# Two more gate blocks by Strassen's algorithm, its products two at a time between the query tiles

## The chip, the cores and the metric

One core of a Trainium2 chip runs the kernel. The metric is device microseconds from start to end of one execution; three runs are given for the kernel before. The core has five engines that work side by side and wait for each other by semaphores: PE (TensorE, matrix products), DVE (VectorE), ACT (ScalarE), POOL (GpSimd) and SP, which issues most of the transfers. Each engine takes its own instructions in the order in which the program gives them.

## The reference

One decoder layer over 256 tokens with a model width of 2048, all in float32. What matters here is the first product and where its columns go:

```
proj = x @ w_in            # 256 x 2048 times 2048 x 15696
q_lat, c_kv, attn_gate, q_idx, k_idx, w_idx, x_rnn, rnn_gate, g_a, g_b = split(proj)
branch_a = (sparse_attention(q_lat, ...) * silu(attn_gate)) @ w_branch_a
branch_b = (rglru(x_rnn) * silu(rnn_gate)) @ w_branch_b
merged   = sigmoid(g_a) * branch_a + sigmoid(g_b) * branch_b
out      = layernorm(ALPHA * x + merged @ w_out)
```

g_a and g_b are the two merge gates, 2048 columns each. The kernel cuts each of them into four blocks of 512 columns, called ga 0 to 3 and gb 0 to 3.

## The kernel before

**Numbers in two parts.** Each float32 operand is split into a high part (a rounded copy, made on ACT by `hi_of`, L106) and a low part (the rest, made on DVE by `lo_of`, L110). A product is three matmuls: high by high, high by low, low by high. x is split once and stays in SBUF as `xs` (16 tiles of 128 rows of the contraction, with 256 high and 256 low columns).

**The weight stream.** All weights pass through one list, `halves`, in pieces of 128 x 1024. `load_to` (L197) gives a piece's transfer to SP; there are four `raw` buffers. `split_to` splits it on ACT and DVE; there are five `hi` and five `lo` buffers. A step of PE asks for splits about five pieces ahead and for loads nine pieces ahead. A buffer comes free when its last reader is done, so a split can't run further ahead than five pieces.

**The order of the work** is written out by hand. `col_jobs` lists the jobs: the rest of qi, ag (attention gate), q (queries), ga 0 to 2, ba (branch A), xr (recurrence input), gb 1 to 3, rg (recurrence gate), bb (branch B); the output product follows. A job of the kinds qi, ag, q, xr, rg makes 128 columns and is run two at a time by `pair`: eight ticks, four in which the high weights meet x (matmuls of 512 columns, L252) and four in which the low weights meet the high part of x (256 columns). A job of the kinds ga, ba, gb, bb is a `chunk`: 16 ticks of six matmuls of 512 columns each (L922 to L924 in `products`), 96 in all. After each tick's matmuls `tick` runs what is due on the other engines: generators sit in an agenda and give up to a later tick at each `yield`. `spawn` puts them there. So attention heads (`head(h)`, spawned 20 ticks after the pair of query tiles it belongs to), drains of PSUM (`evac`, L335 on ACT and L339 on DVE), mask additions on POOL (L509) and the recurrence's `decay` and `roots` all lie beside the weight stream.

**PSUM** has eight banks: four, tag acc, go round among the accumulators of the jobs, and four, tag aux, among everything else (logits, transposes, values).

**What is there of Strassen's algorithm.** ga 3 and gb 0 have the same left operand x, so [ga 3 | gb 0] is taken as a product of 2 x 2 blocks: two halves of the tokens, two halves of the contraction, two column blocks. `quarter_sums` makes the four sums of x's quarters beside ga, `sums` and `split_to` the sums of the weights, `seven_step` runs the seven products within ba 1 to ba 3 in all four aux banks, and `after_s1` and `after_s2` put them together.

**The recurrence.** `decay(n)` for n = 0 to 15 (a tanh and an exp on ACT, then a square on ACT, L759, then a DVE step, L761) starts at tick G0 + 14 + 2n, where G0 is the start of gb 1; `roots(q)` (square roots on ACT, then 16 products on POOL, L770) at G0 + 50 + q. The rg job starts at G0 + 48.

Of the kernel before, what the change touches and what calls it, by code (L numbers as in the profile page):

```python
# [18 lines left out]
P = 128  # L19
# [47 lines left out]

def seven(job):
# [5 lines left out]
            ("ba", 3): ("s2", tuple(range(8)))}.get(job)  # L74

# [7 lines left out]
def layer(ctx, tc, ar, out):  # L83
# [27 lines left out]

    def acc_tile(name):
        return psum.tile([P, 512], F32, name=name, tag="acc", bufs=4)

    def aux_tile(name):
        return psum.tile([P, 512], F32, name=name, tag="aux", bufs=4)

    def slot(name, dt=F32R):
        return big.tile([P, 2 * T], dt, name=name, tag="slot", bufs=16)
# [4 lines left out]
    def gate_tile(name):  # L124
        return gt.tile([P, 2 * T], F32, name=name, tag="gate", bufs=16)
# [26 lines left out]
    causal = const.tile([P, 2, T], F32, name="causal")  # L152
# [12 lines left out]
    for job in jobs:  # L165
# [3 lines left out]
        for pc in range(8 if job[0] in CHUNKS else 2):  # L169
# [5 lines left out]
            halves.append(("w" + job[0], job[1], pc) if job[0] in CHUNKS else ("wt", tiles.index(job), pc))  # L175
    NO = len(halves)
# [4 lines left out]
    def load_to(n):  # L181
        while st["load"] < min(n, len(halves)):
# [7 lines left out]
            raw = wpool.tile([P, 1024], F32, name=f"raw{i}", tag="raw", bufs=4)  # L190
            if kind == "wt":
                src = ar["wt"][a, :, s * 8:(s + 1) * 8, :].rearrange("p k c -> p (k c)")
            elif kind in ("s1a", "s2a"):
# [4 lines left out]
            raws[i] = raw  # L198
# [5 lines left out]
    def sums(i):  # L204

        k, raw = halves[i][1], raws[i]
# [3 lines left out]
    def split_to(n):  # L210
        while st["split"] < min(n, len(halves)):
            i = st["split"]
            kind, k, _ = halves[i]
            if i + 1 < len(halves) and halves[i + 1][0] == "s1a":
# [3 lines left out]
            if NO + 24 <= i < NO + 28:  # L218
                raw = raws.pop(i)
                pieces = []  # L220
                for e in range(2):
                    hi, lo = slot(f"wh{i}_{e}"), slot(f"wl{i}_{e}")
# [5 lines left out]
            else:  # L228
                if kind == "s1b":
                    raw = raws.pop(i - 1)  # L230
                    nc.vector.tensor_sub(raw[:, 512:], form[k], raw[:, :512])
                    src = [(slice(0, 512), form[k]), (slice(512, 1024), raw[:, 512:])]
                elif kind == "s2b":
# [139 lines left out]
    def post_a():  # L373
# [34 lines left out]
        for d in range(2):  # L408
            cT[d] = slot(f"cT{d}")
# [144 lines left out]
    def head(h):  # L554
# [27 lines left out]
        for r in range(2):  # L582
            nc.vector.tensor_scalar(lr[r], lr[r], sm[:, 6 + r:7 + r], None, op0=OP.mult)
# [29 lines left out]
        us[h] = slot(f"ua{h}")  # L613
# [23 lines left out]
    def post_gb(i, pss):  # L637
        for t in range(2):
            g = gates["gb", i, t] = gate_tile(f"gb{i}_{t}")
# [82 lines left out]
    def post_xr(n, ps):  # L722
# [23 lines left out]
        t = ri[n] = slot(f"ri{n}", F32)  # L746
# [5 lines left out]
    def decay(n):  # L752
# [6 lines left out]
        nc.scalar.activation(a2, r, AF.Square)  # L759
# [12 lines left out]
    def post_rg(n, ps):  # L772
# [12 lines left out]
        us[n] = slot(f"ub{n}")  # L785
# [16 lines left out]
    def quarter_sums():  # L802

        x = []
        for j in range(8):
            x.append(gate_tile(f"form{j}"))
# [3 lines left out]
        yield 24  # L810
# [5 lines left out]
        homes = [("qs", "vh"), ("qs", "vl"), ("vh", "vl"), ("bias", "bias", "pa", "pa")]  # L816
        for j in range(4):
            yield 4 if j == 0 else 2
            dst = [p for tag in homes[j] for p in piece(tag, 2, 1 if tag in ("bias", "pa") else 2)]
            first, second = (x[e].rearrange("p (k t) -> p k t", k=2) for e in (j, j + 4))  # L820
            a11, a21, a12, a22 = (v[:, :, c] for v in (first, second) for c in (slice(0, P), slice(P, T)))
            v = [tmp_tile(f"sum{j}_{i}", tag, bufs).rearrange("p (k t) -> p k t", k=2)
# [9 lines left out]
            for i in range(4):  # L832
                lo_of(dst[i][:, :, 1, :], v[i], dst[i][:, :, 0, :])
                for e in range(2):
                    S[i + 1, 2 * j + e] = (dst[i][:, e, 0, :], dst[i][:, e, 1, :])

# [28 lines left out]
    def after_s1():  # L865

        u = {p: att.tile([P, 512], F32, name=f"u{p}", tag="bias", bufs=2) for p in (1, 3)}
        for t in range(2):
            gates["gb", 0, t] = gate_tile(f"gb0_{t}")
        u4, c22 = gates["gb", 0, 0], gates["gb", 0, 1]  # L870
        nc.scalar.activation(u[1], ps7[1], AF.Copy)
# [355 lines left out]
```

## Time and profile before

| | |
|---|---|
| time, median of 3 runs | 1018.04 us (1017.3 to 1018.33) |
| the profiled execution | 1017.16 us; its span, from first to last instruction, 1015.4 us |
| granted TensorE clock | 0.998 of full speed |
| busy over the span | PE 1008.0, DVE 730.9, ACT 569.1, POOL 94.1 us |
| moved by DMA | 205.87 MB, 203 GB/s in the mean |

The profile comes from one execution. A line of it names the source line, the engine, the operation and the tile; matmuls overlap, so their durations are longer than the distance from one start to the next, and it is that distance which adds up to the span. The stages, by the starts of their matmuls: ag from about 65 us, q from 160, ga from 376, ba from 447, xr from 573, gb from 671, rg from 739, bb from 828, the output product from 920.

### The profile page before, as it was taken

The numbers are of one execution on the slowest core, as the hardware profiler recorded it, in microseconds if no ns is written. First come the engines' busy times: TensorE is split into PE (matmuls) and PEld (weight loads), VectorE is DVE, ScalarE is ACT, GpSimd is POOL, SyncE is SP. The second block draws the span as 40 slices with busy tenths as digits, with TensorE's granted clock in tenths as the row PEclk, the third lists the DMA queues.
The fourth block names the chain that finished last, engine by engine and source line by source line (L and its number), as shares of the span: only waits on it lengthen the run. The fifth ranks groups of instructions, "written<-read, shape, count | busy, mean of one in ns | idle before, by whom it ended". The sixth has DMA issues, their size and how long they took to land.

```text
span 1015.4 us, 14822 instructions
## 1 busy us (share of the span) xinstructions
PE 1008.0 (99%) x5344; PEld 870.6 (86%) x5344; DVE 730.9 (72%) x1244; ACT 569.1 (56%) x953; POOL 94.1 (9%) x129
## 2 busy tenths in 40 slices
PE   9999999999999999999999999999999999999997
PEld 8888888899998888888888888888888888888885
DVE  6578885667677766687888688885668875655685
ACT  6566654555555565554555555558866564444452
POOL 0015421110001030000000000000060000000002
PEclk9999999999999999999999999999999999999999
DMA  9755876655565567656776765566745669656652
GB/s 310 255 163 182 296 240 188 200 176 183 173 185 189 177 214 251 187 188 205 220 218 204 228 189 187 189 205 181 207 152 188 206 218 339 197 183 185 202 168 83
DMA packets 62697, 205.87 MB, mean 203 GB/s; under 512 B 6800, under 2 KB 13840, under 8 KB 61600
## 3 DMA queue, kind: packets, MB, share of 16 engines
q1 hardware_dynamic: 59936, 193.23, 60.2%
q0 software_dynamic: 1968, 10.78, 2.9%
q8 instruction: 42, 0.69, 0.3%
q10 hardware_dynamic: 720, 0.92, 0.3%
q14 instruction: 31, 0.25, 0.1%
HBM read 202.77 MB, written 6.32 MB: 206 GB/s over the span
## 4 chain that ended last, share of the span: by engine, by line
PE 99%; DVE 0%; DVEq 0%; issue 0%
PE ps_q L252 17%; PE ps_ag L252 9%; PE ps_xr L252 9%; PE ps_rg L252 9%; PE ps_bb L924 3%; PE ps_bb L923 3%; PE ps_ba L924 3%; PE ps_ba L923 3%; PE ps_ba L922 3%; PE ps_bb L922 3%; PE psq L252 2%; PE ps_qi L252 2%; PE ps_ga L922 2%; PE ps_ga L924 2%; PE ps_gb L922 2%; PE ps_gb L923 2%
## 5 line engine op out<-in xcount | busy, mean ns | idle before, releaser
L110 DVE TENSOR_TENSOR lo<-raw,hi 128x1024 fp32r<-128x1024 f32 x336 | 408.0, 1219 | 234.2 <-ACT hi L106 214.2
L106 ACT ACTIVATE hi<-raw 128x1024 fp32r<-128x1024 f32 x336 | 345.3, 1047 | 128.2 <-PE pso L924 25.3
L252 PE MATMUL ps_q<-xs,hi 128*128 128x512 f32 x512 | 119.0, 390 | 0.0
L252 PEld LDWEIGHTS ps_q<-xs,hi 128*128 128x128 f32 x512 | 95.3, 188 | 19.3
L252 PE MATMUL ps_q<-xs,lo 128*128 128x256 f32 x512 | 69.2, 284 | 0.0
L252 PEld LDWEIGHTS ps_q<-xs,lo 128*128 128x128 f32 x512 | 65.2, 191 | 1.2
L252 PE MATMUL ps_ag<-xs,hi 128*128 128x512 f32 x256 | 60.0, 390 | 0.0
L252 PE MATMUL ps_xr<-xs,hi 128*128 128x512 f32 x256 | 59.6, 390 | 0.0
L252 PE MATMUL ps_rg<-xs,hi 128*128 128x512 f32 x256 | 59.5, 390 | 0.0
L252 PEld LDWEIGHTS ps_xr<-xs,hi 128*128 128x128 f32 x256 | 47.6, 188 | 9.6
L252 PEld LDWEIGHTS ps_rg<-xs,hi 128*128 128x128 f32 x256 | 47.6, 188 | 9.6
L252 PEld LDWEIGHTS ps_ag<-xs,hi 128*128 128x128 f32 x256 | 47.5, 188 | 9.5
L922 PE MATMUL ps_bb<-hi,ub 128*128 128x512 f32 x128 | 50.4, 393 | 0.0
L924 PE MATMUL ps_bb<-hi,ub 128*128 128x512 f32 x128 | 49.9, 390 | 0.0
L923 PE MATMUL ps_bb<-lo,ub 128*128 128x512 f32 x128 | 49.8, 389 | 0.0
L924 PE MATMUL ps_ba<-hi,ua 128*128 128x512 f32 x128 | 49.8, 389 | 0.0
L923 PE MATMUL ps_ba<-lo,ua 128*128 128x512 f32 x128 | 49.8, 389 | 0.0
L922 PE MATMUL ps_ba<-hi,ua 128*128 128x512 f32 x128 | 49.8, 389 | 0.0
L509 POOL TENSOR_TENSOR bias<-bias,mask 128x256 f32<-128x256 f32 (+1 forms) x32 | 24.8, 795 | 195.4 <-DMA bias<-dz 170.3
L922 PE MATMUL ps_ga<-hi,xs 128*128 128x512 f32 x96 | 37.7, 393 | 0.0
L922 PE MATMUL pso<-hi,xs 128*128 128x512 f32 x96 | 37.5, 391 | 0.0
L924 PE MATMUL ps_ga<-hi,xs 128*128 128x512 f32 x96 | 37.4, 390 | 0.0
(358 smaller groups left out, 1971.7 us busy)
## 6 DMA issues: line engine op xcount, KB each, us to landing
raw<-in_wt SPq DMA_DIRECT2D x168, 512.0 KB, 4.8
raw<-in_wba SPq DMA_DIRECT2D x32, 512.0 KB, 3.7
raw<-in_wbb SPq DMA_DIRECT2D x32, 512.0 KB, 4.2
raw<-in_wo SPq DMA_DIRECT2D x32, 512.0 KB, 3.5
raw<-in_wga SPq DMA_DIRECT2D x24, 512.0 KB, 4.5
raw<-in_wgb SPq DMA_DIRECT2D x24, 512.0 KB, 4.5
raw<-in_ws SPq DMA_DIRECT2D x16, 512.0 KB, 4.4
wr<-in_wA SPq DMA_DIRECT2D x14, 424.0 KB, 4.7
```

The costliest lines, as they stand in the source:

```text
L106: nc.scalar.activation(hi, src, AF.Copy)
L110: nc.vector.tensor_sub(lo, src, f(hi))
L252: nc.tensor.matmul(ps[:, :n], w, rhs[:, :n], start=start, stop=stop)
L509: nc.gpsimd.tensor_add(b[:, r, :W[r]], b[:, r, :W[r]], mask[:, r, :W[r]])
L922: nc.tensor.matmul(o, mh, hi, start=first and d == 0, stop=False)
L923: nc.tensor.matmul(o, mh, lo, start=False, stop=False)
L924: nc.tensor.matmul(o, ml, hi, start=False, stop=d == KT - 1)
```

## The change

ga 2 and gb 3 are no longer chunks. [ga 2 | gb 3] is a second product of 2 x 2 blocks with seven products of 24 matmuls (8 tiles of the contraction, three matmuls each). They are run in four phases: j1 (products 1 and 5, eight steps), j2 (3 and 6, eight), j3 (7 alone, four steps of two tiles), j4 (2 and 4, eight). Each step is six matmuls of 512 columns and takes one new piece from the weight stream. `quarters` says after which pair of query tiles the steps stand: none after pairs 0 to 2, two each after 3 to 6, none after 7, then 3, 3, 2, 2, 2, 3, 2, 3 after pairs 8 to 15.

- PSUM: banks get fixed numbers. Banks 3 and 7 are taken out of the two rounds from the end of pair 3 until `after_j4`, one tick into ga; three accumulators and three aux banks are left for the query tiles and the heads.
- x's sums: `early_sums` (three sums, beside pairs 0 to 2) and `late_sum` (the fourth, on POOL, 12 operations, beside pairs 10 to 12). The existing `quarter_sums` moves to ga's now shorter stretch.
- Weight sums: one DVE subtraction of 128 x 512 per step, two in j3.
- Moved between engines: the scaling of the probabilities in `head` from DVE (L583) to ACT, the square in `decay` (L759) from ACT to POOL.
- Moved in time: gb has two chunks, so rg starts at G0 + 32; `decay(n)` starts at G0 + 14 + 4n/3, `roots(q)` at G0 + 37 + q/2.
- The gate tiles and slots are parted into two tags each (gate and form, slot and late); the number of buffers is the same.

```diff
-    jobs += [("ga", i) for i in range(3)] + [("ba", i) for i in range(4)]
+    jobs += [("ga", i) for i in range(2)] + [("ba", i) for i in range(4)]
-    jobs += [("gb", i) for i in range(1, 4)] + [("rg", i) for i in range(16)]
+    jobs += [("gb", i) for i in range(1, 3)] + [("rg", i) for i in range(16)]
...
+def quarters(pair):
+    steps = [("j1", k) for k in range(8)] + [("j2", k) for k in range(8)]
+    steps += [("j3", k) for k in range(4)] + [("j4", k) for k in range(8)]
+    n = (0, 0, 0, 2, 2, 2, 2, 0, 3, 3, 2, 2, 2, 3, 2, 3)
+    return steps[sum(n[:pair]):sum(n[:pair + 1])]
...
+    accs, auxs = [0, 1, 2, 3], [4, 5, 6, 7]
     def acc_tile(name):
-        return psum.tile([P, 512], F32, name=name, tag="acc", bufs=4)
+        accs.append(accs.pop(0))
+        return bank(accs[-1], name)
...
+        if kind == "j1":
+            return nc.vector.tensor_sub(form[k], raw[:, 512:], raw[:, :512])
+        if kind == "j2":
+            return nc.vector.tensor_sub(form[k], raw[:, :512], form[k])
...
-            nc.vector.tensor_scalar(lr[r], lr[r], sm[:, 6 + r:7 + r], None, op0=OP.mult)
+            nc.scalar.activation(lr[r], lr[r], AF.Copy, scale=sm[:, 6 + r:7 + r])
...
-        nc.scalar.activation(a2, r, AF.Square)
+        nc.gpsimd.tensor_mul(a2, r, r)
...
+    def late_sum(j):
+        d, e = (rows2(tmp_tile(f"s3{i}_{j}", "s")) for i in "de")
+        x = [f(xs[:, 2 * j:2 * j + 2, c:c + P]) for c in (0, P, T, T + P)]
+        nc.gpsimd.tensor_sub(d, x[0], x[1])
+        nc.gpsimd.tensor_sub(e, x[2], x[3])
+        nc.gpsimd.tensor_add(d, d, e)
...
+    def quarter_step(job, k):
+        i = where[job, k]
+        split_to(i + 5)
+        load_to(i + 9)
...
+        for e, (p, (mh, ml)) in enumerate(todo):
+            hi, lo = (v[:, e * 512:(e + 1) * 512] for v in parts[i])
+            last = k == (3 if job == "j3" else 7) and (p != 7 or e == 1)
+            nc.tensor.matmul(psj[p], mh, hi, start=k == 0 and (p != 7 or e == 0), stop=False)
+            nc.tensor.matmul(psj[p], mh, lo, start=False, stop=False)
+            nc.tensor.matmul(psj[p], ml, hi, start=False, stop=last)
+        parts.pop(i)
+        split_to(i + 6)
+        load_to(i + 10)
...
+    for j, pair in enumerate((11, 11, 12, 12)):
+        spawn(D0 + 8 * pair - (4 if j < 2 else -1) + j % 2, late_sum(j))
...
-        spawn(G0 + 14 + 2 * n, decay(n))
+        spawn(G0 + 14 + 4 * n // 3, decay(n))
-        spawn(G0 + 50 + q, roots(q))
+        spawn(G0 + 37 + q // 2, roots(q))
...
+        if kind == "q":
+            for job, k in quarters(i // 2):
+                if (job, k) == ("j1", 0):
+                    accs.remove(3)
+                    auxs.remove(7)
+                quarter_step(job, k)
+                if k == (3 if job == "j3" else 7):
+                    spawn(t0 + 8, after[job]())
```

## Rows read from the trace of the kernel before

**Rows 1.** The page: span, busy time of the engines, engines of the chain.

```profile
span 1015.4 us, 14822 instructions
...
PE 1008.0 (99%) x5344; PEld 870.6 (86%) x5344; DVE 730.9 (72%) x1244; ACT 569.1 (56%) x953; POOL 94.1 (9%) x129
...
PE 99%; DVE 0%; DVEq 0%; issue 0%
```

**Rows 2.** Windows q, ba, xr, gb: stretch, length, PE, PEld, DVE, ACT, POOL busy, clock, DMA.

```profile
243.00:296.00 53.00, 53.00 (x327) 47.71 (x326) 37.89 (x89) 30.62 (x70) 4.97 (x8) 1.00 0.59 179
...
469.00:573.00 104.00, 104.00 (x456) 85.47 (x455) 85.50 (x99) 55.32 (x63) 0.00 (x0) 1.00 0.70 213
573.00:678.00 105.00, 105.00 (x622) 93.60 (x621) 85.77 (x146) 58.51 (x97) 1.55 (x16) 1.00 0.61 197
678.00:739.00 61.00, 61.00 (x279) 50.82 (x278) 36.35 (x49) 48.48 (x84) 0.00 (x0) 1.00 0.65 195
```

**Rows 3.** Timeline of PE over gb: start, duration, engine, line, tile.

```profile
670.59 0.40 PE L922 MATMUL ps_gb<-hi,xs 128*128 128x512 f32 x1
...
676.06 0.28 PE L258 MATMUL psg<-xcs,wgh 128*128 128x256 f32 x1
...
676.78 0.39 PE L922 MATMUL ps_gb<-hi,xs 128*128 128x512 f32 x1
...
678.17 0.28 PE L258 MATMUL psg<-xcs,wgh 128*128 128x256 f32 x1
...
738.88 1.29 PE L252 MATMUL ps_rg<-xs,hi 128*128 128x512 f32 x5
```

**Rows 4.** Timeline of PE over one pair of query tiles.

```profile
264.88 7.44 PE L252 MATMUL ps_q<-xs,hi 128*128 128x512 f32 x32
...
272.16 1.11 PE L252 MATMUL ps_q<-xs,lo 128*128 128x256 f32 x8
...
278.06 7.44 PE L252 MATMUL ps_q<-xs,hi 128*128 128x512 f32 x32
```

**Rows 5.** Timeline of DVE around the end of that pair.

```profile
276.50 1.23 DVE L110 TENSOR_TENSOR lo<-raw,hi 128x1024 fp32r<-128x1024 f32 x1 [3.04 <-ACT hi L106]
277.64 0.83 DVE L569 TENSOR_TENSOR bias<-bias,lg 128x128 f32<-128x128 f32 x1
...
281.35 0.41 DVE L339 TENSOR_TENSOR s_q<-ps_q,r_q 128x256 f32<-128x256 f32 x1
```

**Rows 6.** DVE's groups in 199.6 to 358, 160 to 375 and 450 to 573 us.

```profile
L110 DVE TENSOR_TENSOR lo<-raw,hi 128x1024 fp32r<-128x1024 f32 x47 | 57.4, 1228 | 42.7 <-ACT hi L106 39.1 <-PE pspT L588 3.6
...
L583 DVE TENSOR_SCALAR lg<-lg,sm 128x256 f32<-128x256 f32 (+1 forms) x26 | 7.0, 310 | 0.0
...
L110 DVE TENSOR_TENSOR lo<-form,hi 128x512 fp32r<-128x512 f32 x16 | 11.0, 687 | 0.5 <-ACT hi L106 0.3
L208 DVE TENSOR_TENSOR form<-form,raw 128x512 f32<-128x512 f32 x8 | 5.5, 693 | 0.3
```

**Rows 7.** Timeline of DVE and POOL in rg, with and without POOL at work.

```profile
743.34 4.34 POOL L770 TENSOR_TENSOR decay<-decay,ri 128x256 f32<-128x256 f32 x6 [74.85 <-DVE decay L767]
748.93 11.58 POOL L770 TENSOR_TENSOR decay<-decay,ri 128x256 f32<-128x256 f32 x10 [1.25 <-DVE decay L767]
...
755.21 0.96 DVE L780 TENSOR_TENSOR g<-g,s_rg 128x256 f32<-128x256 f32 x1
...
768.10 0.42 DVE L780 TENSOR_TENSOR g<-g,s_rg 128x256 f32<-128x256 f32 x1
```

**Rows 8.** ACT's groups in 693 to 739 us.

```profile
L106 ACT ACTIVATE hi<-raw 128x1024 fp32r<-128x1024 f32 x17 | 17.9, 1054 | 3.5 <-PE ps_gb L924 3.4
L756 ACT ACTIVATE ri<-ri,nc 128x256 f32<-128x256 f32 x16 | 8.2, 510 | 0.5
L755 ACT ACTIVATE decay<-ri,c 128x256 f32<-128x256 f32 x16 | 7.9, 497 | 1.7 <-DVE ri L750 1.7
```

**Rows 9.** The page's DMA issues: size, median us from issue to landing.

```profile
raw<-in_wt SPq DMA_DIRECT2D x168, 512.0 KB, 4.8
```

More of the change, by code (lines that the diff above doesn't have):

```diff
@@ L175, in layer @@
             halves.append(("w" + job[0], job[1], pc) if job[0] in CHUNKS else ("wt", tiles.index(job), pc))
+        if job[0] == "q" and job[1] % 2:
+            for step in quarters(job[1] // 2):
+                where[step] = len(halves)
+                halves.append((*step, 0))
     NO = len(halves)
@@ L197, in load_to @@
             nc.sync.dma_start(raw, src)
-            raws[i] = raw
     form = {}
     def sums(i):
-        k, raw = halves[i][1], raws[i]
+        kind, k, _ = halves[i]
+        raw = raws[i]
+        if kind == "j1":
+            return nc.vector.tensor_sub(form[k], raw[:, 512:], raw[:, :512])
+        if kind == "j2":
+            return nc.vector.tensor_sub(form[k], raw[:, :512], form[k])
+        if kind == "j3":
+            for e in range(2):
+                c = slice(e * 512, (e + 1) * 512)
+                nc.vector.tensor_sub(raw[:, c], form[2 * k + e], raw[:, c])
+            return
+        if kind == "j4":
+            return nc.vector.tensor_sub(raw[:, 512:], form[k], raw[:, :512])
         nc.vector.tensor_sub(raw[:, 512:], raw[:, 512:], raw[:, :512])
@@ L221, in split_to @@
                 for e in range(2):
-                    hi, lo = slot(f"wh{i}_{e}"), slot(f"wl{i}_{e}")
+                    late = i == NO + 27 and e == 1
+                    hi, lo = slot(f"wh{i}_{e}", late=late), slot(f"wl{i}_{e}", late=late)
                     c = raw[:, e * 512:(e + 1) * 512]
@@ L612, in head @@
         yield
-        us[h] = slot(f"ua{h}")
+        us[h] = slot(f"ua{h}", late=h > 13)
         hi_of(us[h][:, :T], u)
@@ L809, in quarter_sums, with four, rows2 @@
                                 ar["xT"][2 * j:2 * j + 2].rearrange("k p t -> p k t"))
-        yield 24
+        return x
+    def four(x, j):
+        first, second = (x[e].rearrange("p (k t) -> p k t", k=2) for e in (j, j + 4))
+        return [v[:, :, c] for v in (first, second) for c in (slice(0, P), slice(P, T))]
+    def rows2(t):
+        return t.rearrange("p (k t) -> p k t", k=2)
+    def quarter_sums():
+        x = load_quarters(1)
+        yield 12
         def piece(tag, bufs, n=1):
@@ new lines, in late_sum @@
+    def late_sum(j):
[4 more added lines that the diff above has]
+        nc.gpsimd.tensor_add(d, d, e)
+        yield 2
+        if j % 2:
+            spare = const.tile([P, 2, T], F32R, name=f"spare{j}", tag="causal", bufs=1)
+            hi, lo = (spare[:, i, :] for i in range(2))
+        else:
+            hi, lo = (ev.tile([P, T], F32R, name=f"s3{i}_{j}", tag="g", bufs=2) for i in "hl")
+        hi, lo = rows2(hi), rows2(lo)
+        hi_of(hi, d)
+        yield
+        lo_of(lo, d, hi)
+        for i in range(2):
+            SJ[3, 2 * j + i] = (hi[:, i, :], lo[:, i, :])
@@ new lines, in after_j4 @@
+    def after_j4():
+        nc.vector.tensor_add(cq["a"], psj[2], cq["a"])
+        yield
+        nc.vector.tensor_sub(cq["b"], cq["b"], psj[4])
+        accs.insert(0, 3)
+        auxs.insert(0, 7)
+        gates["gb", 3, 0], gates["gb", 3, 1] = cq["d"], cq["c"]
+        yield 20
+        for t, n in enumerate("ab"):
+            gates["ga", 2, t] = cq[n]
+            nc.scalar.activation(cq[n], cq[n], AF.Sigmoid)
+            yield
+    after = {"j1": after_j1, "j2": after_j2, "j3": after_j3, "j4": after_j4}
```

147 lines of the change are left out of this document (107 added, 40 removed).

## The prediction

> **What bounds the kernel now.** I read the page first, then the chain of waits, then the windows by stage. The page gives PE 1008.0 us of a span of 1015.4, and the chain that ended last is PE for 99% of its length [rows 1]. The windows say that this is no mean over unlike stages: in q, ba, xr and gb alike PE is busy for the whole stretch and its clock is granted in full [rows 2]. The reader is to see two things in these windows. Time can be won only by taking matmuls away, and any stall put into PE is lost in full. The second thing is how near the others are: DVE fills 71% of q (37.89 of 53.00), and 82% of ba and of xr (85.50 of 104.00, 85.77 of 105.00), and still PE never waits; ACT fills 79% of gb (48.48 of 61.00). So PE's supply holds up to 82% of DVE at least; beyond that this trace shows nothing.
>
> **What PE loses and gains.** The stretch of three gb chunks runs from 670.59 to 738.88, 68.29 us. Four groups of six small matmuls (psg) stand in it, one of them from 676.06 to 676.78, 0.72 us; without them 65.41 us are left for 288 matmuls, 0.2271 us each [rows 3]. Two chunks of 96 go: 192 x 0.2271 = 43.6 us. Added are 28 steps of six such matmuls. Six in a row after a change of form took 1.39 us (676.78 to 678.17) [rows 3], a little more each than in the long run. The steps stand in groups of 12 or 18 after 256-column work, so I take the dearer price: 28 x 1.39 = 38.9 us. The difference is -4.7 us. At the long-run price (168 x 0.2271 = 38.2) it would be -5.4, the best end.
>
> **DVE beside the query tiles.** A pair of query tiles takes 13.18 us (264.88 to 278.06) [rows 4]; at 37.89 of 53.00 us DVE works 9.4 us of it [rows 2]. Moving the scaling to ACT takes off 7.0 us over 13 heads, 0.54 each [rows 6], so 8.9 us. A step of j1 or j2 adds one subtraction of 0.69 us and two low parts of 512 columns at 0.69 [rows 6], 2.1 us against 1.39 us of PE; a step of j4 adds 0.69 and one low part of 1.23, 1.9 us; a step of j3 two subtractions and 1.23, 2.6 us. So a pair with three steps gives DVE 8.9 + 6.2 = 15.1 us in 17.35 of PE (87%). The densest is pair 12: 8.9 + 5.2 for two steps of j3, one closing addition (0.69) and two low parts of the late sums (0.42 each, as a 128 x 256 product without POOL [rows 7]) make 15.6 in 13.18 + 2.78 = 15.96 us (98%). Over pairs 8 to 13 it is six times 8.9, eight steps of j2 (16.6), four of j3 (10.4), three of j4 (5.8), four closing additions (2.8) and four late low parts (1.7): 90.5 of 100.0 us.
>
> **POOL beside DVE.** The late sums and one addition of products put 13 POOL instructions beside pairs 10 to 12. While POOL multiplied in rg, DVE's product on line 780 took 0.96 us; with POOL idle it took 0.42 [rows 7]. So each POOL instruction can cost DVE 0.54 us, 13 of them 7.0, and the dense pairs would stand at 97.5 of 100. The Trainium skill's page "SBUF — State Buffer", section "Who interferes with whom", says that a DVE instruction with two SBUF inputs and a GpSimd instruction that reads SBUF exclude each other for a whole instruction; the trace agrees (0.96 against 0.42). By that rule alone DVE would wait at each meeting, and the result is the first rival below.
>
> Not every one is met. The late sums of tiles 0 and 1 start before DVE's pause (3.04 us in front of the low part at 276.50 [rows 5]); that pause is theirs. Those of tiles 2 and 3 fall at the head of pair 12, where DVE has a queue: six times 0.54, 3.2 us, and 15.6 + 3.2 is 2.9 over PE's 15.96. The splits run up to five pieces ahead, so most of that is taken from the lead. Bounds of the stall that reaches PE in the whole stage: 0 (as at 82%) and 3.7 (first rival). I take 0.7, a quarter of the overrun, nearer to the rows in which PE never waited.
>
> **Three accumulators instead of four.** The second accumulator of a pair is now the bank of the first accumulator of the pair before, and PE wants it half way through the four high ticks, 3.64 us (half of 264.88 to 272.16 [rows 4]) after the pair before has ended, plus 1.39 us per step between. Its drain by DVE starts at 281.35 and takes 0.41 [rows 5]: 3.70 us after the pair's end at 278.06. With no step between (pair 7) that is even, -0.06 us. With two steps PE comes 2.7 us after the drain; with three, one more subtraction and the split low part stand ahead of the drain (0.84 us) and 3.3 us are left. Cost 0.1 us at most; the price without the cover is the second rival.
>
> **ACT, transfers and the queues.** ACT works 30.62 of 53.00 us in q [rows 2], 7.6 per pair; three steps add three high parts at 1.05 [rows 8] and the scaling 0.54 by DVE's row and at most twice that, at most 11.9 of 17.35: hidden. The scaling's result is read three ticks later, where ACT has its own waits. Between three steps and the next pair seven pieces are split in one stretch, but there are four raw buffers and a transfer lands 4.8 us after its issue [rows 9]. The fourth piece of the next pair is wanted 4.17 + 5.5 us after the pair's end, and its buffer comes free 2 to 3 us after it, so it is there with about 2 us over; the stall term holds what of this goes wrong. SP issues the heads' bias loads behind these pieces, a pair ahead of their use; at nothing.
>
> **gb and rg.** From G0 + 14 to G0 + 32 PE has 18 ticks of six matmuls, 24.5 us. In it ACT has 14 decays at 1.01 (0.51 + 0.50) and nine high parts at 1.05 [rows 8], 23.6 us, and the drains of a chunk. It is full but not over, since the square has gone to POOL. What slips goes into the four high ticks of the first rg pair (7.28 us [rows 4], one split), ahead of the roots. I take 0; if that cover is gone, the two decays that no longer fit ahead of rg come first, 2.0 us. Sixteen squares on POOL cost DVE up to 0.54 each in a stretch where it works 36.35 of 61.00 us [rows 2]: hidden.
>
> **The sum.** -4.7 + 0.7 = -4.0 us on the profiled execution of 1017.16, 1013.2. The median of the three runs, 1018.04, lies 0.9 above that execution, so the forecast for a median is 1014.0.
>
> **The rivals.**
> 1. *DVE becomes the bound between pairs 8 and 13, and the gain is spent there.* For it: 90% without POOL, 97.5% with it, and DVE's forced pauses (42.7 us in front of the low parts in twelve pairs [rows 6], 3.6 each, of which some depend on PE and ACT in turn). Against it: these pauses are mostly lead, not need. If 1.2 us of pause per pair stay forced, 97.5 + 7.2 = 104.7 against 100.0; a lead of about 1 us is used up first, so 3.7 are lost: -1.0, about 1017.0.
> 2. *The drain of the first accumulator comes too late at every pair.* PE then waits for DVE, DVE's next work waits for PE, and nothing is caught up. It decides where DVE runs some 3 us later at the end of a pair than now. For it: 0.06 us of shortage without steps, and a stage at 90%. Against it: 2.7 to 3.3 us of room at ten of the eleven seams. At 1 us for each of eleven seams: +11.0 - 4.7 = +6.3, about 1024; above 0.43 us per seam the change loses.
> 3. *ACT is late into rg.* For it: 23.6 of 24.5 us; against it: the quiet high ticks. -4.0 + 2.0, about 1016.0.
>
> **How the numbers follow.** The forecast has 0.68, rival 1 0.15, rival 2 0.10, rival 3 0.07. 0.2% is 2.0 us, about what a measurement can tell here. Faster by more: the forecast and half of rival 3, 0.71. Slower by more: rival 2 and a little of what goes beyond rival 1, 0.11. The rest, 0.18, is within. The range starts at the best end (1018.04 - 5.4) with 0.3 for the spread of runs, 1012.3, and takes in rivals 3 and 1 up to 1018.0; rival 2 and the far end of rival 1 are left out.
>
> **What would show it.** The page has 5320 matmuls (24 fewer), and PE busy about 4 us less. The step groups take 1.39 us per step with no gap. DVE is at 85 to 98% in pairs 8 to 13, and PE's idle time there is under 1.5 us in all: if it is more, the releaser tells rival 1 (a low part, `hi` or `lo`) from rival 2 (the drain `s_q`). The subtraction takes 0.69 us alone. In rg's first two pairs PE has no gap; a gap ended by an ACT high part is rival 3. The forecast is wrong if PE's idle time grows by more than 2 us anywhere, or if the steps take over 1.5 us each.

## The result, and the profile after

The changed kernel takes 1027.49 us in the median of 4 runs (1026.22 to 1028.04), the kernel before 1017.68 beside it: ratio 1.0094, 95% interval 1.0076 to 1.0111. Forecast were 1014.0 us and faster. It is slower, by 9.5 us where 4.0 were to be won. (In the experiments one of the ten runs of `e8_five` took 1482.52 us at a granted clock of 0.632; it is left out, so that the median told here is 1018.60 and not the 1018.96 of the expectations.)

The page of the changed kernel, the lines that answer to [rows 1]:

```profile
span 1025.8 us, 14984 instructions
...
PE 1006.9 (98%) x5320; PEld 867.4 (85%) x5320; DVE 780.7 (76%) x1306; ACT 594.9 (58%) x1014; POOL 127.9 (12%) x166
...
PE 87%; DVE 5%; ACT 4%; issue 2%; DMA 1%; POOL 0%; DVEq 0%; ACTq 0%; POOLq 0%
```

The 24 matmuls are gone, as forecast, and the chain that ended last is no longer PE alone: DVE, ACT and DMA hold a tenth of it. What PE waited for in the changed kernel (in all us, times, longest; the kernel before has none of these seven):

```profile
PE psl L305 <- DVE cq_b L994: 5.2, 1, 5.2
PE pspv L650 <- DVE vl L120: 2.8, 1, 2.8
PE psj L961 <- DVE pb L120: 1.3, 1, 1.3
PE psj L962 <- DVE lo L120: 1.1, 1, 1.1
...
PE ps_rg L299 <- ACT hi L116: 0.6, 1, 0.6
...
PE psj L961 <- ACT hi L116: 0.3, 1, 0.3
PE ps_ga L1096 <- DVE lo L120: 0.3, 1, 0.3
```

Seven waits, 11.6 us. By stage, from the starts of the first matmuls (us); the two columns on the right are experiments told below:

| stage | before | changed | `e14_roots_spaced` | `e18_j3_unsubtracted` |
|---|---|---|---|---|
| q, with the 28 steps | 216.2 | 260.9 | 256.7 | 254.4 |
| ga (3 chunks before, then 2) | 71.2 | 57.2 | 50.1 | 50.1 |
| ba | 126.1 | 126.2 | 126.2 | 126.2 |
| xr | 97.5 | 97.5 | 97.5 | 97.5 |
| gb (3 chunks before, then 2) | 68.3 | 46.5 | 46.5 | 46.5 |
| rg | 88.9 | 90.1 | 90.0 | 89.9 |

gb gives back 21.8 us for one chunk; ga should too and gives 14.0. The price of a step, in the changed kernel's timeline of PE (the answer to [rows 3]): 18 matmuls, three steps, and then the next pair.

```profile
290.57 0.40 PE L961 MATMUL psj<-hi,sj 128*128 128x512 f32 x1
...
294.67 0.62 PE L299 MATMUL ps_q<-xs,hi 128*128 128x512 f32 x2
```

4.10 us, 1.37 per step; 28 steps are 38.3 us. So q should be 216.2 + 38.3 = 254.5 and is 260.9. The losses are 6.4 us in q, 7.8 in ga and 1.3 in rg; 15.5 less the 43.6 - 38.3 = 5.3 of matmuls won is 10.2, and the spans differ by 10.4. Within q the loss lies in three pairs of query tiles: 1.6 us in pair 3, 3.1 in pair 11, 1.9 in pair 12. Each of the other thirteen takes its time of the kernel before and 1.37 us per step, within 0.05 us.

The engines over three stretches of q (the columns of [rows 2]):

```profile
243.00:296.00 53.00, 53.00 (x304) 46.75 (x303) 42.30 (x90) 35.12 (x74) 5.88 (x8) 1.00 0.59 189
296.00:349.00 53.00, 50.25 (x290) 44.31 (x289) 43.48 (x81) 35.15 (x74) 11.32 (x14) 1.00 0.60 186
349.00:402.00 53.00, 51.64 (x295) 45.03 (x295) 45.94 (x88) 32.87 (x67) 11.04 (x11) 1.00 0.61 187
```

DVE is at 80, 82 and 87%. In the first stretch PE never waits, in the second, at 82%, it loses 2.75 us. In the kernel before, PE never waited at 82% in ba and xr [rows 2]. The share does not tell the two apart. By pairs it tells still less; here are pair 11 and pair 13, each with its steps:

```profile
330.57:349.54 18.97, 16.22 (x95) 14.20 (x94) 15.76 (x27) 11.19 (x23) 4.34 (x4) 1.00 0.58 181
...
367.36:384.67 17.31, 17.31 (x100) 15.26 (x99) 16.97 (x35) 11.16 (x23) 2.15 (x2) 1.00 0.62 185
```

With DVE at 83% pair 11 loses 2.75 us; with DVE at 98% pair 13 loses nothing. What tells them apart is the chain. The chain of the changed kernel through pair 11 (start, us, what):

```profile
329.05 2.28 DVE lo L120 x2
...
331.35 5.28 DMA raw<-in_wga
...
336.71 1.29 DVE raw L247 x2
338.01 1.14 DVE lo L120
...
340.47 1.40 DVE qs L120
...
342.21 0.61 DVE vl L120
...
342.86 0.50 PE pspv L650
```

Read backwards: `pspv` wants an aux bank that still holds the values `psv`; the bank is free when DVE has written `vl`; `vl` stands in DVE's queue behind a split, and that behind a subtraction (L247) that waited for its weight piece, which landed 5.28 us after the buffer had come free. DVE's own timeline between 332 us and `vl` at 342.13 says what makes it late: 1.33 and 0.50 us of idle time for two landings, 2.4 us of subtractions for two pieces, and `qs`, which takes 1.48 us beside POOL's addition to `cq_c` where the next `qs` takes 0.41. The chain at the start of ga is of the same kind:

```profile
421.19 7.41 DMA raw<-in_wga
...
428.70 1.06 ACT hi L116
...
429.79 1.23 DVE lo L120
431.02 0.60 DVE cq_a L992
...
432.68 0.61 DVE cq_b L994
...
433.33 0.58 PE psl L305
```

`after_j4` puts bank 7 at the head of the aux round, so head 14's logits (`psl`) get it, and it still holds product 4 until `cq_b` has been written, behind a split that waited for a landing of 7.41 us. What stood beside that landing is in the timelines of POOL and SP in 414 to 434 us:

```profile
416.54 5.82 POOL L855 DMA_DIRECT2D form<-in_xT  x8
```

```profile
416.30 15.07 SPq L229 DMA_DIRECT2D raw<-in_wga  x7
```

x's quarters (2 MB) are sent for beside seven weight pieces. In 420 to 430 us the DMA engines are at a share of 1.00 and move 365 GB/s (177 in the 18 us before).

This burst is not new. The kernel before sends for the same 2 MB at the same place, one tick later in ga (POOL, L808, from 373.60 us). Its weight pieces there take up to 7.1 us to land, and PE does not wait:

```profile
380.00:385.00 5.00, 5.00 (x30) 4.40 (x29) 2.90 (x9) 2.64 (x5) 0.00 (x0) 1.00 1.01 374
385.00:390.00 5.00, 5.00 (x26) 4.08 (x25) 5.00 (x11) 2.91 (x6) 0.35 (x1) 1.00 1.00 343
```

New in the changed kernel is that a bank which PE wants at once is drained behind such a landing.

### The profile page after: what moved, and what is told of

It reads as the page before. It is cut to its first block, busy times and chain, and to the rows that moved or that the text cites. A ratio compares the mean times of both kernels' runs of the same rounds, so it can differ in the third digit from the quotient of the medians.

```text
span 1025.8 us, 14984 instructions
## 1 busy us (share of the span) xinstructions
PE 1006.9 (98%) x5320; PEld 867.4 (85%) x5320; DVE 780.7 (76%) x1306; ACT 594.9 (58%) x1014; POOL 127.9 (12%) x166
## 4 chain that ended last, share of the span: by engine, by line
PE 87%; DVE 5%; ACT 4%; issue 2%; DMA 1%; POOL 0%; DVEq 0%; ACTq 0%; POOLq 0%
PE ps_q L299 15%; PE ps_ag L299 9%; PE ps_xr L299 9%; PE ps_rg L299 5%; PE ps_ba L1096 3%; PE ps_bb L1096 3%; PE ps_bb L1095 3%; PE ps_ba L1097 3%; PE ps_ba L1095 3%; PE ps_bb L1097 3%; PE psq L299 2%; PE ps_qi L299 2%; PE pso L1095 2%; PE pso L1096 2%; PE pso L1097 2%; DVE lo L120 2%
## 5 line engine op out<-in xcount | busy, mean ns | idle before, releaser
L120 DVE TENSOR_TENSOR lo<-raw,hi 128x1024 fp32r<-128x1024 f32 x348 | 418.4, 1209 | 185.8 <-ACT hi L116 170.5
L116 ACT ACTIVATE hi<-raw 128x1024 fp32r<-128x1024 f32 x348 | 350.2, 1029 | 166.7 <-PE pso L1097 25.3
L556 POOL TENSOR_TENSOR bias<-bias,mask 128x256 f32<-128x256 f32 (+1 forms) x32 | 27.0, 865 | 191.4 <-DMA bias<-dz 75.1
L1095 PE MATMUL pso<-hi,xs 128*128 128x512 f32 x96 | 37.5, 391 | 0.0
L1097 PE MATMUL pso<-hi,xs 128*128 128x512 f32 x96 | 37.4, 389 | 0.0
L1096 PE MATMUL pso<-lo,xs 128*128 128x512 f32 x96 | 37.4, 389 | 0.0
```

What stands on the lines that cost most here:

```text
L116: nc.scalar.activation(hi, src, AF.Copy)
L120: nc.vector.tensor_sub(lo, src, f(hi))
L556: nc.gpsimd.tensor_add(b[:, r, :W[r]], b[:, r, :W[r]], mask[:, r, :W[r]])
L1095: nc.tensor.matmul(o, mh, hi, start=first and d == 0, stop=False)
L1096: nc.tensor.matmul(o, mh, lo, start=False, stop=False)
L1097: nc.tensor.matmul(o, ml, hi, start=False, stop=d == KT - 1)
```

## The experiments

Theory after the comparison: every large wait is for a PSUM bank whose drain stands, in order, behind a split that waits for a landing; there are fewer banks to go round, and at ga's start the landings are slow. Rival: DVE has too much work between the pairs, whatever the order.

**e1: both held banks to the end of their rounds.**

```diff
-        accs.insert(0, 3)
-        auxs.insert(0, 7)
+        accs.append(3)
+        auxs.append(7)
```

> One edit to the changed kernel: after j4 the two borrowed PSUM banks go to the end of the rounds, not to their head, so that head 14's logits no longer ask for the bank that DVE has yet to drain. Theory (PE waits for drains of PSUM banks that come round too soon; the biggest such wait, 5.2 us for cq_b, then costs about 2 us more at the lower clock): that wait and the lowered clock vanish, about 7.5 us less than the changed kernel, near 1020.0. Rival (the weight pieces of ga come late by DMA and DVE whatever the banks do): PE waits for hi or lo of ga instead, at most 3 us are won, 1024.5 or more.

1029.29 us (1.0110, 1.0095 to 1.0125). A miss: psl's wait is gone, but the edit made another in its place, `ps_ga` for ScalarE's `ga`, 4.6 us, because the second chunk of ga now took the bank that the first had just filled.

**e2: x's quarters later.**

```diff
-    spawn(at["ga", 0] + 3, quarter_sums())
+    spawn(at["ga", 0] + 9, quarter_sums())
     x = load_quarters(1)
-    yield 12
+    yield 6
```

> One edit to the changed kernel: the transfer of x's quarters (2 MB on the POOL queue) starts six ticks later, at tick 9 of ga, and the sums that need it stay where they are. Theory (the burst of DMA at ga's start, 344 to 385 GB/s from 420 to 430 us, makes the pieces land late, so the splits and behind them the drain cq_b are late): with the burst gone cq_b comes 4 us or more earlier, the wait on the bank shrinks to under 1.5 us and the clock stays up: 1020 to 1023.5. Rival (DVE simply has too much work at this seam): the wait stays above 4 us, 1026 or more.

1022.73 us (1.0044, 1.0029 to 1.0059), 4.8 below the changed kernel. Its first waits of PE:

```profile
PE pspv L650 <- DVE vl L120: 2.1, 1, 2.1
PE psl L305 <- DVE cq_b L994: 1.7, 1, 1.7
```

psl's wait goes from 5.2 to 1.7 us with the bank order untouched, and ga takes 5.3 of its lost 7.8 us less. So the drain behind a slow landing makes most of ga's loss; the burst alone cost the kernel before nothing.

**e3: the steps hold the two oldest banks** instead of 3 and 7.

```diff
-                    accs.remove(3)
-                    auxs.remove(7)
+                    held[0] = accs.pop(0)
+                    held[1] = auxs.pop(0)
```

> One edit to the changed kernel: the two banks taken for the products are the ones whose last use lies longest back, not always banks 3 and 7. Theory: the 1.3 us that the first step of j1 waits for DVE's drain pb vanish and no other wait grows: 1026.2. Rival (DVE is behind by its amount of work, and PE meets the same lateness at the next wait): no change, 1027.5.

1025.75 us (1.0078, 1.0063 to 1.0093), 1.7 below, though the two intervals overlap. In the trace the wait for `pb` is gone and pair 3 loses nothing any more; the large waits stay.

**e4: each subtraction right before its own split** instead of one piece ahead.

```diff
-            if i + 1 < len(halves) and halves[i + 1][0] in ("s1a", "j1", "j2", "j3", "j4"):
+            if kind in ("j1", "j2", "j3", "j4"):
+                load_to(i + 1)
+                sums(i)
+            if i + 1 < len(halves) and halves[i + 1][0] == "s1a":
```

> One edit to the changed kernel: the weight subtraction of a step of j1 to j4 stands right in front of its own split and no longer one split ahead, so DVE, which works in order, meets the piece's transfer one split later. Theory (DVE stands at a subtraction until its piece has landed, and the drains behind it come late): DVE's waits for in_wga and in_wj before line 241 to 250 (1.33, 0.50, 0.88 us) vanish, the PE wait for vl in pair 11 (2.8 us) falls to 1 us or less: 1025.5. Rival (the amount of DVE work in pairs 8 to 13, not the order, holds the drain up): the wait for vl stays above 2 us, 1027 or more, and ACT's high parts now wait for the subtraction.

1035.08 us (1.0165, 1.0148 to 1.0182), 7.6 above the changed kernel. The expectation failed: the waits for `vl` (1.6 us) and `cq_b` (3.9 us) shrank by little over 1 us each, and psj now waits for ScalarE's `hi` (3.2 us) and DVE's `lo` (2.2 us), since ScalarE finds nothing subtracted ahead of it.

**e5: only the aux bank to the end of its round.**

```diff
-        auxs.insert(0, 7)
+        auxs.append(7)
```

> The first experiment's edit, halved: only the aux bank goes to the end of its round after j4; the accumulator's bank goes to the head as in the changed kernel, so ga 1 doesn't take the bank that ga 0 has just filled. Theory (waits for PSUM banks): the 5.2 us at head 14's logits and the lowered clock go, the wait of 1.5 us for head 14's scaled probabilities stays: 1021.5. Rival (the lateness of DVE and ACT at this seam is met at the next wait whatever the banks): the waits at ga's start stay above 5 us in sum, 1026 or more.

1023.10 us (1.0054, 1.0039 to 1.0069), 4.4 below; psl's wait is gone, and 2.3 us of it come back at `pspT`, behind ScalarE's `lg`.

**e6: the values' drain ahead of the next split,** in `values`.

```diff
-        split_to(i + 6)
-        load_to(i + 10)
...
                 hi_of(hi[:, s, :], pss[s])
-            yield
             for s in range(2):
                 lo_of(lo[:, s, :], pss[s], hi[:, s, :])
             vs[g] = (hi, lo)
+            yield
```

> One edit to the changed kernel: the drain of the values' banks (vh on ACT, vl on DVE) stands ahead of the next split in both queues; no work is added or removed. Theory (DVE works in order and vl stood behind j3's subtractions, which stood waiting for their transfers): the wait of PE for vl (2.8 us) falls under 0.5 us: 1025. Rival (DVE has too much work in pairs 8 to 13): the same time is met at a low part or another drain, 1027 or more.

1028.59 us (1.0100, 1.0082 to 1.0118): the wait for `vl` is gone, `pspT` waits 1.0 us for `lg` instead, psj 0.8 for `hi`. No gain.

**e7: the late sum in one buffer,** three operations on POOL as before.

```diff
-        nc.gpsimd.tensor_sub(e, x[2], x[3])
-        nc.gpsimd.tensor_add(d, d, e)
+        nc.gpsimd.tensor_add(d, d, x[2])
+        nc.gpsimd.tensor_sub(d, d, x[3])
```

> One edit to the changed kernel: a late sum is added up in one buffer (x0 - x1 + x2 - x3, still three POOL operations) and no longer in two, so the last of them doesn't wait for a buffer that the query tiles' drain holds. Theory (buffer wait of 7.9 us on POOL makes the fourth sum late, ACT and the split of the piece behind it too): the waits of PE in pair 12 (1.1 and 0.3 us) go: 1026.1. Rival (POOL's instructions slow DVE by 0.54 us each, and that is what is late): no change, 1027.5.

1026.86 us (1.0085, 1.0070 to 1.0100), 0.6 below, within the spread of the two.

**e8: e2, e3, e5, e6 and e7 together.**

> Five edits together: aux bank to the end of the round, x's quarters six ticks later, oldest banks for the products, the values' drain first, one buffer for a late sum. Theory (each stall has its own place and cause, and they add): 7.5 + 1.3 + 2.8 + 1.4 us less than the changed kernel, 1014.5. Rival (a common cause, DVE's work at 90% and over, that comes out at whatever wait is next): 1018 or more.

1018.60 us (1.0009, 0.9999 to 1.0018), 8.9 below the changed kernel.

**e9: the same without e6.**

> Four of the five edits of the run before: the two banks that the steps held go to the end of their rounds (aux) as in the fifth run, x's quarters are sent for later, the steps hold the two oldest banks, and the late sum uses one buffer. What is left out is the values' drain ahead of the next split, which alone gained nothing (1028.59 against 1027.49). The theory (each stall of TensorE is a PSUM bank whose drain on VectorE or ScalarE stands behind a split that waits for a weight piece to land) expects about what the five gave, 1018 to 1020, with the wait of psl gone and vl at 1 to 2 us. The rival that VectorE as a whole is too full expects no gain from moving banks at all, above 1025, which the five's 1018.96 already speaks against; if the values' drain does matter once the other waits are gone, this run is 1 to 2 us above the five.

1017.09 us (0.9992, 0.9983 to 1.0001), 10.4 below the changed kernel and level with the kernel before. The four alone gave 4.8, 1.7, 4.4 and 0.6, 11.5 in all; e2 and e5 mend the same wait, so they can't add up fully. With e6 besides (e8) it is 1.5 above this, and the same 1.5 lies between e10 and e11 below. The expectation did not have that: the earlier drain of the values costs.

**e10 and e11: decays and roots placed otherwise,** on e9 and on e8.

```diff
-        spawn(G0 + 14 + 4 * n // 3, decay(n))
+        spawn(G0 + 14 + 9 * n // 8, decay(n))
-        spawn(G0 + 37 + q // 2, roots(q))
+        spawn(G0 + 34 + q // 2, roots(q))
```

> The same four edits, and in the last phase the decays and the roots on ScalarE are spread so that they begin a little earlier and closer (steps of 9/8 of a slot instead of 4/3 for the decays, the roots three slots earlier). The theory that the last phase lost 1.26 us because ScalarE comes late with hi into rg expects 0.6 to 1.3 us below the four (1017.5 to 1019). The rival, that the loss there comes from the weights' own lateness and not from ScalarE's queue, expects no difference from the four.

> All five edits and the spread of the decays: 0.6 to 1.3 us below the five, so 1017.6 to 1018.4, if ScalarE's lateness into rg is what is left there; unchanged at 1019 by the rival. To be faster than the kernel before (1017.7) it would have to keep all of the 4.7 us of matmuls but some 2 us, which I hold for possible but not likely.

1017.12 us (0.9996, 0.9987 to 1.0005) and 1018.57 (1.0006, 0.9997 to 1.0015). No gain: rg's wait for `hi` is 1.2 us in both instead of 0.6. The times are as the rival had them; its reason is not shown, since PE still waits for ScalarE's `hi` there.

**e12: 16 of the subtractions carried out twice,** on the changed kernel.

```diff
-            return nc.vector.tensor_sub(form[k], raw[:, 512:], raw[:, :512])
+            for _ in range(2):
+                nc.vector.tensor_sub(form[k], raw[:, 512:], raw[:, :512])
+            return
```

(and the same for j4)

> The changed kernel, with 16 of its 28 subtractions of weights (those of the first and the last of the four products' groups) carried out twice, 16 x 0.69 = 11.0 us more of VectorE between the query tiles, with the same transfers and the same result. The theory that VectorE has room (80 to 87% busy there) and is late only because it waits for pieces to land expects the doubled ones to fall into idle time but where a bank waits behind them: +0 to +3 us on 1027.5. The rival that VectorE's amount of work is the bound of these pairs expects most of the 11 us in the time: +7 to +11, 1034 to 1038.

1032.24 us (1.0139, 1.0125 to 1.0153): 4.8 of the 11.0 us reach the time, which is between the two expectations. Its waits:

```profile
PE psl L309 <- DVE cq_b L998: 6.8, 1, 6.8
PE psj L965 <- DVE pb L120: 2.5, 1, 2.5
PE psj L966 <- DVE lo L120: 1.7, 2, 1.3
PE pspv L654 <- DVE vl L120: 1.3, 2, 0.9
```

The 16 are half of 32 subtractions (a step of j3 has two), and they run in pairs 3 to 6 and 13 to 15, not in 11 and 12. Pairs 5 and 6 now have DVE at 92% (31.74 of 34.52 us) and lose nothing; pair 3 loses 4.2 us instead of 1.6. The added work shows at a few places, not as a bound all over q. So DVE's amount of work matters, but only where a bank waits behind it: neither theory was right alone.

**e13: two of POOL's places in pairs 11 and 12.** On e9: the late sum takes one of `r`'s buffers instead of `s`'s, and POOL's addition to `cq_c` becomes one on DVE, some ticks later.

```diff
-        d = rows2(tmp_tile(f"s3d_{j}", "s"))
+        d = rows2(tmp_tile(f"s3d_{j}", "r"))
-        nc.gpsimd.tensor_add(cq["c"], cq["c"], cq["b"])
-        yield 8
+        yield 5
+        nc.vector.tensor_add(cq["c"], cq["c"], cq["b"])
+        yield 3
```

> The four edits of the ninth run, and in pairs 11 and 12: the late sum takes one of r's buffers instead of one of s's (in the ninth run GpSimd stood 10.8 us for s's, until VectorE's qs at 358.5, and TensorE then waited 1.0 us for lo behind it), and GpSimd's sum of cq_c, 1.44 us beside which VectorE's qs took 1.49 us instead of 0.41, ahead of vl, becomes an addition on VectorE some slots later (about 0.69 us). The theory that these two places hold what is left of the query stage's stalls (2.1 for vl, 1.0 for lo) expects 1.5 to 2.5 us below the ninth run's 1017.1: 1014.6 to 1015.6, with the lo wait gone and vl at about 1 us, since the 5.2 us landing ahead of it stays. The rival that the landings of the weights alone set these waits expects no change from 1017.

1018.49 us (1.0008, 0.9999 to 1.0017), 1.4 above e9: a miss. The wait for `lo` is gone, but POOL, no longer held up, now works beside DVE's subtractions. Timeline of POOL and DVE in e13:

```profile
350.73 1.71 POOL L924 TENSOR_TENSOR s3d<-xs 128x256 f32<-128x256 f32 x1
351.77 2.37 DVE L247 TENSOR_TENSOR raw<-form,raw 128x512 f32<-128x512 f32 x2
...
353.67 1.08 POOL L926 TENSOR_TENSOR s3d<-s3d,xs 128x256 f32<-128x256 f32 x1
354.06 1.76 DVE L120 TENSOR_TENSOR lo<-raw,hi 128x1024 fp32r<-128x1024 f32 x1
355.75 1.28 DVE L247 TENSOR_TENSOR raw<-form,raw 128x512 f32<-128x512 f32 x2
```

Two such subtractions take 2.37 us beside POOL and 1.28 without. The chain goes through these DVE lines on to `cq_d`, `sm`, ScalarE's scaling `lg` and `pspT`, for which PE now waits 1.6 us.

**e14: ScalarE's roots one tick apart,** on e9, and **e15: e13 and e14 together.**

```diff
-        spawn(G0 + 37 + q // 2, roots(q))
+        spawn(G0 + 37 + q, roots(q))
```

> The four edits of the ninth run, and ScalarE's four square roots one slot apart instead of two by two, with a split's hi between each (8 us of roots and two table loads as before). The theory that the last phase's 1.2 us (0.6 on matmuls and 1.5 on weight loads, both for ScalarE's hi) comes from hi standing behind two roots at a time expects 0.6 to 1.2 us below the ninth run: 1015.9 to 1016.5. The rival that ScalarE is full there from 716 to 745 us whatever the order (two chunks of gb instead of three stand over the same decays) expects the wait moved to the next hi, and 1017.

> Both: if the stalls are where I place them and add up, 1013.6 to 1015, so 0.9960 to 0.9973 of the kernel before, which would be the forecast's matmul term (4.7 us) less about 1.5 us of stall left. If only the landings count, 1016.5 to 1017.

e14: 1016.94 us (0.9993, 0.9984 to 1.0002); rg's wait is 0.4 instead of 0.6, and against e9 nothing that can be told apart. (e9, e10 and e14 are the same up to the end of q, yet PE waits there for 3.1, 2.4 and 1.7 us in their profiles: single waits differ by that much between executions.) e15: 1018.72 us (1.0010, 1.0001 to 1.0019); e13's loss stays.

**e16: none of the change's tensor work in the pairs on POOL,** on e14: the late sums' 12 operations and the addition to `cq_c` (as in e13) are on DVE.

```diff
-        nc.gpsimd.tensor_sub(d, x[0], x[1])
-        nc.gpsimd.tensor_add(d, d, x[2])
-        nc.gpsimd.tensor_sub(d, d, x[3])
+        nc.vector.tensor_sub(d, x[0], x[1])
+        nc.vector.tensor_add(d, d, x[2])
+        nc.vector.tensor_sub(d, d, x[3])
```

> The fourteenth run (the four edits and the roots spaced, 1016.94), with the late sums' twelve operations and the sum of cq_c on VectorE instead of GpSimd: 12 x 0.42 + 0.69 = 5.7 us more of VectorE's own work, and no GpSimd operation of the change beside VectorE's any more. In the thirteenth run, where GpSimd's late sums ran earlier, VectorE's work beside them took 3.11 instead of 2.46, 2.37 instead of 1.29 and 1.76 instead of 1.22 us, and the run was 1.4 us above the ninth, not below. The theory that this contention, not the order of the buffers, holds the stalls of pairs 11 and 12 expects the lo wait of pair 12 (0.8 to 1.0) gone and no wait of pspT in its place: 1014.5 to 1016. The rival that the weights' landings (5.2 us before pair 11's second subtraction) set the waits, and any more work on VectorE lengthens them, expects 1017 to 1019.

1017.63 us (0.9997, 0.9988 to 1.0006), 0.7 above e14. The waits in q are `lo` 1.0, `lg` 0.9, `vl` 0.6, 2.5 us in all, within what e9, e10 and e14 show among themselves. Contention of the late sums with DVE is gone, 5.7 us of DVE's own work stand in its place, and nothing is won that can be told apart.

**e17: the steps' pieces queued four ahead instead of five,** on e14.

```diff
+            if i >= n - 1 and i + 1 < len(halves) and halves[i + 1][0][0] == "j":
+                return
```

> The fourteenth run (four edits, roots spaced, 1016.94), with the subtraction and split of each of the steps' pieces put into the engines' queues one piece later: four pieces ahead of its use instead of five, so that VectorE, which works in order, comes to the wait for a landing later and the drains of pairs 11 and 12 (cq_b, vl, pa) stand ahead of it. The theory that the last stalls are drains queued behind a subtraction that waits for a landing (1.3 us at pair 11, 5.2 us from issue to landing) expects vl's 0.9 and some of lo's 0.8 gone: 1015.3 to 1016.5. The rival that five pieces ahead are needed, because hi and lo of the steps' pieces come too late with fewer, expects waits of psj for lo or hi in its place and 1017.5 to 1020, as when each subtraction stood right before its own split (7.6 us slower).

1023.02 us (1.0056, 1.0042 to 1.0070), 6.1 above e14, as the rival had it. The wait for `vl` is gone, and in its place:

```profile
PE psj L965 <- DVE lo L120: 2.3, 3, 0.9
PE psj L964 <- ACT hi L116: 1.6, 1, 1.6
PE ps_ga L1099 <- DVE lo L120: 1.1, 1, 1.1
```

**e18: without j3's eight subtractions,** on e14.

```diff
         if kind == "j3":
-            for e in range(2):
-                c = slice(e * 512, (e + 1) * 512)
-                nc.vector.tensor_sub(raw[:, c], form[2 * k + e], raw[:, c])
             return
```

> The fourteenth run (four edits, roots spaced, 1016.94) without the eight subtractions of j3's weights (8 x 0.69 = 5.5 us of VectorE in pairs 11 and 12): product 7 is taken with the weights as they are loaded, so the gates' blocks are not the reference's. Loads, buffers, splits and matmuls stay. VectorE then has nothing in its queue that waits for a landing itself; only ScalarE's high part does. The theory that the last stalls of pairs 11 and 12 are drains behind VectorE's subtraction and its wait expects vl's 0.9 and lo's 0.8 gone and 1015.0 to 1016.0. The rival that the pieces come too late for TensorE in any case (four buffers, 4.5 to 5 us a landing) expects the wait moved to psj for hi or lo, or to vl behind lo, and 1016.5 to 1017.

1014.31 us (0.9964, 0.9951 to 0.9978), 2.6 below e14, for a kernel that leaves out a part of the work. Windows over pairs 11 and 12, first of e14, then of e18 (columns as in [rows 2]):

```profile
326.00:345.00 19.00, 18.10 (x103) 15.78 (x102) 16.33 (x32) 12.08 (x25) 4.45 (x6) 1.00 0.63 191
345.00:364.00 19.00, 18.24 (x104) 15.65 (x103) 16.16 (x30) 10.97 (x24) 6.96 (x7) 1.00 0.56 180
```

```profile
326.00:345.00 19.00, 19.00 (x108) 16.65 (x107) 15.94 (x28) 12.92 (x25) 5.99 (x7) 1.00 0.67 202
345.00:364.00 19.00, 19.00 (x108) 16.64 (x107) 16.48 (x33) 11.84 (x24) 4.43 (x5) 1.00 0.59 200
```

PE's 1.66 us of idle time are gone, and q takes 254.4 us, which is 216.2 for the query tiles and 38.2 for 28 steps. The transfers are the same as in e14, so landings alone do not hold these last stalls: it takes DVE's subtraction in front of the drain. In pair 11 the traces tell its work from its wait. DVE ahead of `vl`, first in e14, then in e18:

```profile
332.21 1.29 DVE L247 TENSOR_TENSOR raw<-form,raw 128x512 f32<-128x512 f32 x2 [1.28 <-DMA raw<-in_wga]
```

```profile
333.54 1.23 DVE L120 TENSOR_TENSOR lo<-raw,hi 128x1024 fp32r<-128x1024 f32 x1 [1.25 <-ACT hi L116]
```

DVE still stands idle there for 1.25 us, now for ScalarE's `hi`, which waited for the same piece to land. What is gone is the 2.4 us of subtractions for two pieces, and `vl` starts 1.6 us earlier in the pair (8.1 us after its start instead of 9.7), although `qs` takes 1.1 us longer beside POOL. So in pair 11 it is the subtractions' work ahead of the drain, and not a wait of their own, that e18 takes away. For pair 12 this is not shown.

## Why the prediction was wrong

- **The matmul term, -4.7, was right.** gb gives 21.8 us for its chunk, the steps cost 1.37 us each where I had taken the dearer 1.39, and the term is -5.3. With the stalls out of q, e18 comes to 1014.31. That this is near the forecast's 1014.0 is luck: e18 leaves out eight subtractions, and 0.6 us of ga's loss and 1.0 of rg's are still in it.
- **The stall term, +0.7 with bounds of 0 and 3.7, is the step that failed.** It measured 6.4 us in q and 7.8 in ga. It was made from DVE's share of a pair, with the overrun "taken from the lead". DVE's amount of work was forecast well: 91.7 us over pairs 8 to 13, where the prediction has 90.5 without POOL and 97.5 with it. PE waited all the same, in pairs 11 (83%) and 12 (81%) and not in pair 13 (98%). A drain is late because of all that stands ahead of it in DVE's queue: subtractions, waits for a landing or for ScalarE, and an operation that POOL slows. In pair 12 it is a split's own `lo` and `hi` that come late.
- **Of the banks I followed only the accumulators.** There I was right: no `ps_q` waits, and rival 2 as I put it, at every seam, did not happen. But the change took one of four aux banks too, and the waits for `psl`, `pspv` and the first step of j1 are for those. The mechanism of rival 2 came about in the banks that I had not looked at. (No run keeps all four aux banks, so that a fourth would end the wait for `vl` is not shown.)
- **The values were left out of the dense stretch.** Its 100.0 us are six pairs of 13.18 us and 15 steps. Pair 10 takes 15.94 us in the kernel before, because it also makes values, and the drain of these, `vl`, is what PE waited for in pair 11.
- **ga stood in no term of the sum.** The prediction did not ask who takes the returned bank first, nor what its drain stands behind: weight pieces that land slowly beside x's quarters, as they already did in the kernel before. That is 7.8 us: 5.2 of wait, 0.3 for `lo`, and most of the rest at a lower clock (below). e2 and e5 mend it from either side, each worth over 4 us alone.
- **"There with about 2 us over" failed at pair 11.** DVE stood idle for two landings (one of 5.28 us instead of 4.8), 1.83 us in all, and two j3 pieces have 2.4 us of subtractions.
- **Rival 1** had the right size for what is left once the banks and the burst are mended: 2.2 us lie in pairs 11 and 12 between the traces of e14 and e18, and e9 and e14 are at 1017, the time that it gave. That the time agrees is in part luck: DVE was no bound over pairs 8 to 13, and its work counted only in two of them. The sign that the prediction named, the releaser, points both ways there: 2.8 us of the changed kernel's waits are for a drain (`vl`), 1.4 for `lo` and `hi`.
- **POOL beside DVE** is as dear as [rows 7] say or dearer (1.07 us on `qs` from one addition of 128 x 512), but it is not the bound: with the change's operations off POOL (e16) nothing was won.
- **gb and rg, 0 or else 2.0:** 1.3 lost. ScalarE was late, as rival 3 has it, and by less; two other placings (e10, e14) did not change the time.

So the -4.7 are there, and the change gives them and 10 us more to stalls. With the four edits it stands level with the kernel before; no version with all of its subtractions was shown to be faster. What would free pairs 11 and 12 with the subtractions in place stays open: e13, e16 and e17 did not. No run takes back the scaling's move to ScalarE, whose `lg` PE waits for in e5, e6, e13 and e16, or the square's move to POOL.

## What to carry to other kernels

Before adding work between matmuls, list for each PSUM bank who takes it next and what stands, in order, ahead of its drain on the draining engine; the engine's busy share does not show that (here 83% with a stall, 98% without). Where a bank is taken out of a round or given back, and where a load is moved, go through the first user on the other side as for a new instruction: here the wait at the returned bank was the largest of all, 5.2 us, behind landings that had been slow before at no cost. Work on weights that are just landing stands, wait and all, ahead of the drains of the engine that does both.

## What the runs showed of the hardware

TensorE's clock fell in the changed kernel's wait at ga. Windows of two us (columns as above; the clock is the third number from the end):

```profile
428.00:430.00 2.00, 0.11 (x1) 0.00 (x0) 0.21 (x1) 1.30 (x2) 0.00 (x0) 1.00 1.02 391
430.00:432.00 2.00, 0.00 (x0) 0.00 (x0) 2.00 (x5) 1.79 (x8) 0.00 (x0) 0.59 0.89 354
432.00:434.00 2.00, 0.67 (x3) 0.67 (x4) 1.27 (x4) 1.81 (x5) 0.00 (x0) 0.50 0.91 306
434.00:436.00 2.00, 2.00 (x10) 1.96 (x10) 1.89 (x3) 1.16 (x3) 0.26 (x1) 0.50 0.44 116
436.00:438.00 2.00, 2.00 (x9) 1.71 (x8) 2.00 (x5) 0.53 (x2) 1.87 (x2) 0.71 0.84 213
```

PE stands from 428.1 to 433.3 us; the granted clock goes from 1.00 (2.4 GHz) to 0.50 (1.2 GHz) and is back at 1.00 after 438. Work from 433.3 to 436 at half speed and from 436 to 438 at 0.71 loses, as worked out from these shares, 1.3 + 0.6 = 1.9 us on top of the wait. The 2.8 us of pair 11 brought no such fall: the stretch around it is granted 1.00.

A weight piece that lands in 4.8 us in the median (`in_wt`) took 7.41 us beside the 2 MB of x's quarters, at 365 GB/s and a DMA share of 1.00, and up to 7.1 us beside the same 2 MB in the kernel before.

POOL and DVE slow each other in both directions: two subtractions 2.37 against 1.28 us, and POOL's 128 x 256 operation 1.71 us where it took 0.74 in e9. The Trainium skill's page "SBUF — State Buffer", section "Who interferes with whom", says that the port pair which the two share is an exclusive lock, and that a DVE instruction with two SBUF inputs contends with a GpSimd instruction that reads SBUF. The trace agrees in that both lose time here; for how long one holds the other is not shown.
